# Causal branch of a two-layer backbone: norms one block ahead, turned keys' copies queued first, backward loads a block ahead, an update copied by ScalarE

## The chip, the cores and the metric

One core of a Trainium2 chip runs the whole program. The metric is device time in microseconds (us) of one execution. A core has a matrix engine (TensorE, PE in the profile; PEld are its weight loads), VectorE (DVE), ScalarE (ACT), GpSimd (POOL) and SyncE (SP), which here issues all the DMAs. Each engine works through its own queue in order and waits at its head.

## The reference

Two layers run over 2048 latent and 256 context tokens of width 1024. A layer normalises its tokens, modulates them, projects them to 3584 columns, runs four branches, and projects back with a gated residual. The branch that the change touches is a recurrence with 4 heads of 64 keys and 64 values, run once forward and once backward over the tokens, context first:

```
def step(state, inp):                       # one chunk of 64 positions
    a = jnp.cumsum(lf, axis=2)              # running log of the forget gate f
    s_new = exp(a_last) * state + einsum("bhsk,bhsv->bhkv", kc * exp(a_last - a), vc)
    inter = einsum("bhtk,bhkv->bhtv", qc * exp(a), state)
    dec = exp(where(causal, diff, -inf))    # diff = a at t minus a at s, causal: s <= t
    scores = einsum("bhtk,bhsk,bhtsk->bhts", qc, kc, dec)
    return s_new, inter + einsum("bhts,bhsv->bhtv", scores, vc)
```

The sum of both directions goes through an RMS norm per head. Inputs, weights and output are float32.

## The kernel before

Tokens are handled in 18 tiles of 128 rows, two to a block, so in 9 blocks; block 0 is the context. The kernel is written with a scheduling layer: the program is traced in an order, and a compile-time scheduler then sorts the instructions of every engine's queue by that order and by its own estimate of when each is ready. What is traced earlier has priority. Waits between engines are semaphores that the layer adds; two engines never use one PSUM bank at the same time. The traced order comes from `weave` (L41): each stream is a generator with a count of units and a span, and the stream whose next unit has the lowest relative place goes next. `after(i)` (L94) puts what is traced inside it behind instruction `i` on `i`'s own engine.

The stages of a layer that matter here:

1. **The forward stage** (L1427 to L1464; in layer 0 about 75 to 375 us of the trace, in layer 1 about 1434 to 1748 us). For each block `sb`, three streams are woven: `hg_proj(sb)` projects the block's queries, two directions' forget gates and values (L441 to L443 and L455 to L457, three fp16 products for one float32 product); `hg_levels(sb-1)` works on the block before; and `norms(sb)` normalises the two tiles of the block two ahead, in the span 0.3 to 1.0. Two blocks' tiles, 2 to 5, are normalised ahead of the loop (L1450 and `run(norms(0))`). A norm of one tile is `norm_front` (load L329 into one of two buffers `nh`, square on ScalarE L332, scaling on VectorE L336) and `norm_turn` (two groups of four TensorE transposes L353, each followed by four ScalarE modulations L360, then a cast L364 and a difference L365 on VectorE).
2. **Within `hg_levels`** keys K and queries Q are multiplied by products of forget gates over spans of 1, 2, 4, ..., 64 positions (levels `B`). At each level VectorE multiplies one half of the columns (L600, L603) and ScalarE copies the other half (L606, L607, "level copies", four for keys and queries together). TensorE forms scores from pairs of levels (`hg_scores`, L716), which are evacuated into Sd and Sx (L559 to L564). Then, for each of the block's two 128-row chunks `ch`: four TensorE transposes of the keys (L649), a ScalarE copy of them to SBUF (`kut`, L651, "key copy", one buffer), the products keys times values of both directions (L664) and the outputs (L673) into two PSUM banks `po` of the tag `sc`, which has two in all. The banks are then emptied: ScalarE copies outputs (L689), VectorE updates the forward state (`hg_state`, L475, two instructions), copies the backward direction's update to `dsb` (L692) and the gate product (L693), and adds the second bank (L695). Outputs and backward queries are stored to DRAM (L696, L697). The products L664 of the second chunk need the second key copy and both banks free.
3. **The last block** of the forward stage is woven with two blocks of `gate_block` for weight column 13 (48 products each, L455 to L457).
4. **The backward stage** (`hg_reverse`, about 375 to 470 us and 1745 to 1835 us): for each block, in the order 0, 8, 7, ..., 1, it loads stored queries (L739) and outputs (L740), multiplies the queries by the state (L750), updates the state (L475), adds, normalises and stores (L771). It is woven with the other gate blocks, Fourier blocks, weight preparation and, in layer 0, with modulation columns of 1 MB weight loads.

Of the kernel before, what the change touches and what calls it, by code (L numbers as in the profile page):

```python
# [12 lines left out]
F32 = mybir.dt.float32  # L13
# [13 lines left out]
NTT = NT // 128  # L27
KC = D // 128
DEPTH = 2
# [11 lines left out]
def weave(*streams):  # L41

    live = []
    for n, gen, *span in streams:
        a, b = span or (0.0, 1.0)
        live.append([0, n, gen, a, b - a])
    while live:
        e = min(live, key=lambda x: x[3] + x[4] * (x[0] + 0.5) / x[1])
        try:
            next(e[2])  # L50
            e[0] += 1
        except StopIteration:
            live.remove(e)
# [6 lines left out]
def run(gen, n=None):  # L60

    for i, _ in enumerate(gen):
        if i + 1 == n:
            break
# [8 lines left out]
class Net:  # L73
# [388 lines left out]
    def hg_open(self, l, keep):  # L462
        nc = self.nc

        self.hst = [self.t(keep, [128, 2, 64], F32, f"hst{i}", 1) for i in range(3)]
        for s in self.hst:
            nc.gpsimd.memset(s, 0.0)
        self.hcur = 0
        self.dsb = self.t(keep, [128, NTT, 2, 64], F32, "dsb", 1)
        self.fbc = self.t(keep, [128, NTT, 2], F32, "fbc", 1)  # L470

# [58 lines left out]
    def hg_levels(self, l, sb, hp):  # L530

        nc = self.nc
# [36 lines left out]
        while B <= 64:  # L569
            D_ = N // B  # L570

            F2 = self.t(hp, [128, 3 * (D_ // 2) + 8], F32, f"hF{2 * B}", 1)
            nc.vector.tensor_mul(
                out=F2[:, : 3 * D_ // 2], in0=F[:, 0 : 3 * D_ : 2], in1=F[:, 1 : 3 * D_ : 2]
            )
            if need and len(group) == 2:
                if pend:
                    keep()
                pend = self.hg_scores(group)
                group = []  # L580

            def fpair(base, step, n):

                v = F[:, base : base + 2 * step].rearrange("p (r q) -> p r q", r=2)
                return v[:, :, 0 : 4 * (n - 1) + 1 : 4].rearrange("p r n -> p n r")

            if B < 64:
                n4 = N // (4 * B)
                for X, Y, tag, (ob, os), (ib, is_) in (
                    (Kc, Ky, "hK", (1, D_ + 1), (D_, D_ + 3)),  # L590
                    (Qc, Qy, "hQ", (D_ + 1, D_ + 1), (0, D_ + 3)),
                ):
                    if X is None:
                        continue
                    Xn = self.t(hp, [128, N], F32, tag + "c", 3)
                    Yn = self.t(hp, [128, N], F32, tag + "y", 2)
                    v4 = lambda a: a.rearrange("p (n j b) -> p n j b", j=4, b=B)
                    x4, y4, xn, yn = v4(X), v4(Y), v4(Xn), v4(Yn)
                    sh = [128, n4, 2, B]
                    nc.vector.tensor_tensor(  # L600
                        out=xn[:, :, 0::3], in0=x4[:, :, 0::3], in1=fpair(ob, os, n4).unsqueeze(3).to_broadcast(sh), op=ALU.mult
                    )
                    nc.vector.tensor_tensor(  # L603
                        out=yn[:, :, 1:3], in0=x4[:, :, 1:3], in1=fpair(ib, is_, n4).unsqueeze(3).to_broadcast(sh), op=ALU.mult
                    )
                    nc.scalar.copy(out=xn[:, :, 1:3], in_=y4[:, :, 1:3])  # L606
                    nc.scalar.copy(out=yn[:, :, 0::3], in_=y4[:, :, 0::3])  # L607
                    if tag == "hK":
                        Kc, Ky = Xn, Yn
                    else:  # L610
                        Qc, Qy = Xn, Yn
                if need:
                    group.append((2 * B, Kc, Qc))
            else:
                res = []
                v2 = lambda a: a.rearrange("p (n j b) -> p n j b", j=2, b=64)
                fv = lambda d, e: F[:, d * D_ : d * D_ + D_].rearrange("p (n j) -> p n j", j=2)[:, :, e].unsqueeze(2).to_broadcast([128, 4, 64])
                for X, Y, tag, spec in (
                    (Kc, Ky, "hK", ((0, 0, 1), (1, 1, 0))),
                    (Qc, Qy, "hQ", ((1, 0, 0), (0, 1, 1))),  # L620
                ):
                    if X is None:
                        res += [None, None]
                        continue
                    for (half, d, e), tg in zip(spec, ("c", "y")):
                        Z = self.t(hp, [128, N], F32, tag + tg, 3 if tg == "c" else 2)
                        nc.vector.tensor_tensor(out=v2(Z)[:, :, half], in0=v2(X)[:, :, half], in1=fv(d, e), op=ALU.mult)
                        nc.scalar.copy(out=v2(Z)[:, :, 1 - half], in_=v2(Y)[:, :, 1 - half])
                        res.append(Z)
            F = F2  # L630
            B *= 2
            yield
            if B > 2:
                yield
# [7 lines left out]
        for ch in range(2):  # L642
# [5 lines left out]
                    x = (i * 2 + g) * 128  # L648
                    nc.tensor.transpose(pt[:, x : x + 128], c4(a, g), self.id32)  # L649
            kut = self.t(hp, [128, 512], F32, "hkut", 1)  # L650
            nc.scalar.copy(out=kut, in_=pt)  # L651
            yield
            yield

# [13 lines left out]
            if need:  # L668
# [19 lines left out]
                            mm(a, b, h, (Sd if a == b else Sx)[p, h % 2, ch * 2 + h // 2], it[p, ch, h * 64 : h * 64 + 64], h == 3)  # L688
                nc.scalar.copy(out=dv[:, ch], in_=po[0][:, 0:256])  # L689
            u = po[0][:, 256:512].rearrange("p (d g v) -> p d g v", d=2, g=2)  # L690
            self.hg_state(new, old, FC[:, 0, :, ch], u[:, 0])
            nc.vector.tensor_copy(out=self.dsb[:, tt], in_=u[:, 1])  # L692
            nc.vector.tensor_copy(out=self.fbc[:, tt], in_=FC[:, 1, :, ch])  # L693
            if need:
                nc.vector.tensor_add(out=dv[:, ch], in0=dv[:, ch], in1=po[1][:, 0:256])  # L695
# [27 lines left out]
    def hg_reverse(self, l, pool):  # L723
# [7 lines left out]
        for s in st:  # L731
            nc.gpsimd.memset(s, 0.0)
        cur = 0
        for sb in [0] + list(range(NTT // 2 - 1, 0, -1)):
            need = l < DEPTH - 1 or sb > 0
            if need:
                qb = self.t(pool, [128, 2, 256], F32, "hKc", 2)
                o = self.t(pool, [128, 2, 256], F32, "hQc", 2)
                nc.sync.dma_start(out=qb, in_=self.d_qb[sb * 2 : sb * 2 + 2].rearrange("c p x -> p c x"))  # L739
                nc.sync.dma_start(out=o, in_=self.d_op[sb * 256 : sb * 256 + 256].rearrange("(c p) x -> p c x", p=128))  # L740
                po = self.bank("pv", cols=1024)
            for ch in (1, 0):
                tt = sb * 2 + ch
# [647 lines left out]
    def layer(self, l, L, R, tail):  # L1391
# [35 lines left out]
        with ExitStack() as st:  # L1427
            hp = self.pool(st, "hg", "left")
            self.hin = {}
            block = self.hg_proj(l, 0, hp)  # L1430
            if l == 0:
                w = [self.wprep(l, b, quick=True) for b in (8, 9, 10)]
                with self.after(last):
                    run(w[0], 2)
                    run(w[1], 2)
                    run(w[2], 1)
                run(block, 8)
                for i in range(3):
                    run(w[i])
                    with self.after(*self.wlast):  # L1440
                        if i == 0:
                            run(w[2], 1)
                        run(block, 1 if i == 0 else 8)
                self.load_masks()
            else:
                self.wlast = ()
            self.hg_open(l, hgk)
            nc.gpsimd.memset(self.omx, 0.0)
            with self.after(*self.wlast):
                for tt in (2, 3):  # L1450
                    self.norm_tile(l, tt, nm)

            def norms(sb):
                for tt in (2 * sb + 4, 2 * sb + 5):
                    if tt < NTT:
                        h = self.norm_front(l, tt, nm)
                        yield
                        yield from self.norm_turn(l, tt, h, nm)

            run(block)  # L1460
            run(norms(0))
            for sb in range(1, NS):
                weave((33, self.hg_proj(l, sb, hp)), (22, self.hg_levels(l, sb - 1, hp)), (8, norms(sb), 0.3, 1.0), *([(7, self.wprep(l, 13), 0.4, 0.8)] if sb == NS - 1 else []))
            weave((22, self.hg_levels(l, NS - 1, hp)), chain(*gates(13, 512, some[:2])))  # L1464


        def late():
# [17 lines left out]
        with ExitStack() as st:  # L1485
            rp = self.pool(st, "rv", "left")
            streams = [
                (NS, self.hg_reverse(l, rp)),
                chain(*gates(13, 512, some[2:]), *[(9, self.fourier_block(sb, 12)) for sb in some]),
                (21, preps((12, 6, 4))[1], 0.1, 1.0),  # L1490
            ]
            if l == 0:
                streams.append((33, self.adaln_rest(self.pool(st, "ada", "left")), 0.1, 1.0))
            weave(*streams)
# [210 lines left out]
```

## Time and profile before

| | |
|---|---|
| median of 3 runs | 2701.15 us (2696.48 to 2701.3) |
| profiled execution, its own time | 2704.5 us |
| its span in the trace | 2701.9 us |
| PE busy | 2559.8 us, 95% of the span |
| PEld / DVE / ACT / POOL busy | 1914.5 / 2168.8 / 1476.1 / 106.1 us |
| mean granted TensorE clock | 0.982 |

The span is the time from the first to the last instruction of the program; the profiled execution's own time is 2.6 us longer. An engine's busy time is the union of its instructions, so TensorE is not idle for more than about 142 us in all.

### The profile page before, as it was taken

The numbers are of one execution on the slowest core, as the hardware profiler recorded it, in microseconds if no ns is written. First come the engines' busy times: TensorE is split into PE (matmuls) and PEld (weight loads), VectorE is DVE, ScalarE is ACT, GpSimd is POOL, SyncE is SP. The second block draws the span as 40 slices with busy tenths as digits, with TensorE's granted clock in tenths as the row PEclk, the third lists the DMA queues.
The fourth block names the chain that finished last, engine by engine and source line by source line (L and its number), as shares of the span: only waits on it lengthen the run. The fifth ranks groups of instructions, "written<-read, shape, count | busy, mean of one in ns | idle before, by whom it ended". The sixth has DMA issues, their size and how long they took to land. (4 is left out here: it accounts for less than half of the span.)

```text
span 2701.9 us, 67158 instructions
## 1 busy us (share of the span) xinstructions
PE 2559.8 (95%) x28046; PEld 1914.5 (71%) x28046; DVE 2168.8 (80%) x4771; ACT 1476.1 (55%) x2725; POOL 106.1 (4%) x108
## 2 busy tenths in 40 slices
PE   5899999999899999999999999999998999999998
PEld 3788877878777775555547788888886777555553
DVE  5888865677689889987878888778788988998875
ACT  2877642322225556788847666433221555798882
POOL 0000001001000000000000000010110000000000
PEclk7999999999999999999999999999999999999999
DMA  6111158353331005242372111243434100424325
GB/s 220 57 49 49 38 161 275 124 150 102 99 81 44 25 25 148 81 117 85 102 208 85 45 49 36 87 131 130 140 100 109 40 25 17 122 59 126 110 63 140
DMA packets 268679, 260.31 MB, mean 96 GB/s; under 512 B 95316, under 2 KB 237656, under 8 KB 268376
## 3 DMA queue, kind: packets, MB, share of 16 engines
q1 hardware_dynamic: 268376, 256.04, 31.8%
q8 instruction: 219, 3.59, 0.6%
q14 instruction: 84, 0.69, 0.1%
HBM read 168.59 MB, written 67.13 MB: 87 GB/s over the span
## 5 line engine op out<-in xcount | busy, mean ns | idle before, releaser
L441 PE MATMUL psmm<-xh,wh 128*128 128x256 f16 x2208 | 607.5, 275 | 10.3 <-DVE xh L364 6.1
L442 PE MATMUL psmm<-xl,wh 128*128 128x256 f16 x2208 | 606.2, 275 | 1.6 <-DVE xl L365 1.6
L443 PE MATMUL psmm<-xh,wl 128*128 128x256 f16 x2208 | 606.2, 275 | 0.9 <-DVE wl L417 0.9
L1034 ACT ACTIVATE aP<-pssc,pshift,ascale 128x512 f32<-128x512 f32 (+1 forms) x584 | 447.9, 773 | 242.8 <-PE pssc L1032 207.2
L455 PE MATMUL psmm<-wh,xh 128*128 128x256 f16 x1664 | 459.3, 276 | 10.3 <-ACT av L828 8.6
L457 PE MATMUL psmm<-wh,xl 128*128 128x256 f16 x1664 | 458.9, 276 | 0.0
L456 PE MATMUL psmm<-wl,xh 128*128 128x256 f16 x1664 | 458.7, 276 | 0.0
L1041 DVE TENSOR_TENSOR apl<-aP,aph 128x512 f16<-128x512 f32 (+1 forms) x584 | 394.0, 681 | 79.7 <-ACT aph L1040 74.4
L957 DVE TENSOR_REDUCE amx<-pstr 128x1 f32<-128x512 f32 (+1 forms) x648 | 390.1, 627 | 45.9 <-PE pstr L956 44.0
L998 PE MATMUL pspv<-V,aph 128*128 128x129 f16 x2320 | 289.6, 221 | 0.1
L999 PE MATMUL pspv<-V,apl 128*128 128x65 f16 x2320 | 267.5, 193 | 10.5 <-DVE apl L1041 9.8
L1040 ACT CAST aph<-aP 128x512 f16<-128x512 f32 (+1 forms) x444 | 269.3, 613 | 10.9
L999 PEld LDWEIGHTS <-apl 128*128 128x128 f16 x2320 | 207.5, 98 | 82.4 <-DVE apl L1041 27.8
L442 PEld LDWEIGHTS <-wh 128*128 128x128 f16 x2208 | 217.5, 99 | 66.3 <-issue 11.1
L441 PEld LDWEIGHTS <-wh 128*128 128x128 f16 x2208 | 217.7, 99 | 65.3 <-issue 12.4
L998 PEld LDWEIGHTS <-aph 128*128 128x128 f16 x2320 | 214.4, 97 | 57.9 <-ACT aph L1040 1.4
L956 PE MATMUL pstr<-K,Q 128*128 128x512 f16 (+1 forms) x648 | 228.4, 357 | 17.5 <-DVE amx L957 7.3
L443 PEld LDWEIGHTS <-wl 128*128 128x128 f16 x2208 | 217.3, 98 | 37.2 <-issue 2.6
L1031 PE MATMUL pssc<-Q,K 128*128 128x512 f16 (+1 forms) x584 | 220.4, 377 | 8.1 <-ACT aP L1034 6.6
L1032 PE MATMUL pssc<-Q,K 66*128 66x512 f16 (+1 forms) x584 | 221.0, 379 | 0.0
L1321 PE MATMUL psmm<-xh,oyh 128*128 128x512 f16 x544 | 207.9, 382 | 7.6 <-DMA oyh<-oa 5.6
L1321 PE MATMUL psmm<-xl,oyh 128*128 128x512 f16 x544 | 207.9, 382 | 0.0
(308 smaller groups left out, 4249.9 us busy)
## 6 DMA issues: line engine op xcount, KB each, us to landing
wst<-w_in SPq DMA_DIRECT2D x56, 512.0 KB
wmod<-w_mod SPq DMA_DIRECT2D x18, 1024.0 KB
d_G<-nh SPq DMA_DIRECT2D x51, 256.0 KB
oo<-d_O SPq DMA_DIRECT2D x34, 384.0 KB
og<-d_G SPq DMA_DIRECT2D x34, 384.0 KB
d_h<-oh SPq DMA_DIRECT2D x18, 512.0 KB
nh<-d_h SPq DMA_DIRECT2D x18, 512.0 KB
nh<-x SPq DMA_DIRECT2D x16, 512.0 KB
```

The lines of the kernel that those rows point to most:

```text
L441: nc.tensor.matmul(out, lhsT=wh[:, k, cs], rhs=a, start=(k == 0), stop=False)
L442: nc.tensor.matmul(out, lhsT=wh[:, k, cs], rhs=b, start=False, stop=False)
L443: nc.tensor.matmul(out, lhsT=wl[:, k, cs], rhs=a, start=False, stop=(k == KC - 1))
L455: nc.tensor.matmul(out, lhsT=a, rhs=wh[:, k, :], start=(k == 0), stop=False)
L456: nc.tensor.matmul(out, lhsT=a, rhs=wl[:, k, :], start=False, stop=False)
L457: nc.tensor.matmul(out, lhsT=b, rhs=wh[:, k, :], start=False, stop=(k == KC - 1))
L957: nc.vector.tensor_reduce(out=mx[:, h, j, i : i + 1], in_=ps[:, :w], axis=AX.X, op=ALU.max)
L998: nc.tensor.matmul(pv(j), lhsT=ph[:, t], rhs=self.V[:, s, kv, :], start=st, stop=False, skip_group_check=True)
L999: nc.tensor.matmul(pv(j)[:, 0:65], lhsT=pl[:, t], rhs=self.V[:, s, kv, 0:65], start=False, stop=sp and j % 2 == 1, skip_group_check=True)
L1034: nc.scalar.activation(out=P[:, :n], in_=ps[:, :n], func=AF.Exp, scale=self.ascale, bias=self.pshift)
L1041: nc.vector.tensor_sub(out=pl[:, :n], in0=P[:, :n], in1=ph[:, :n])
L1321: nc.tensor.matmul(ps, lhsT=y, rhs=w, start=(i == 0), stop=(i == len(mms) - 1))
```

## The change

Four things change. The norms of a block are traced one block ahead of their use instead of two, so that only tiles 2 and 3 are normalised ahead of the loop, and within a block they take the span 0.05 to 0.75 instead of 0.3 to 1.0. The level copies of the first two levels of a block are queued on ScalarE behind the last key copy of the block before. The copy of the backward update (`dsb`) goes from VectorE to ScalarE, ahead of the state update. In the backward stage the loads of a block are traced one block earlier, with a unit of their own ahead of the first block. A third gate block moves from the backward stage into the weave of the last forward block.

```
-        self.hcur = 0
+        self.hcur, self.kutlast = 0, []
...
-                    nc.scalar.copy(out=xn[:, :, 1:3], in_=y4[:, :, 1:3])
-                    nc.scalar.copy(out=yn[:, :, 0::3], in_=y4[:, :, 0::3])
+                    with self.after(*self.kutlast) if B < 4 else ExitStack():
+                        nc.scalar.copy(out=xn[:, :, 1:3], in_=y4[:, :, 1:3])
+                        nc.scalar.copy(out=yn[:, :, 0::3], in_=y4[:, :, 0::3])
...
-            nc.scalar.copy(out=kut, in_=pt)
+            self.kutlast = [nc.scalar.copy(out=kut, in_=pt)]
...
             u = po[0][:, 256:512].rearrange("p (d g v) -> p d g v", d=2, g=2)
+            nc.scalar.copy(out=self.dsb[:, tt], in_=u[:, 1])
             self.hg_state(new, old, FC[:, 0, :, ch], u[:, 0])
-            nc.vector.tensor_copy(out=self.dsb[:, tt], in_=u[:, 1])
...
-        for sb in [0] + list(range(NTT // 2 - 1, 0, -1)):
+        order = [0] + list(range(NTT // 2 - 1, 0, -1))
+
+        def load(sb):
+            if l == DEPTH - 1 and sb == 0:
+                return None
+            qb = self.t(pool, [128, 2, 256], F32, "hKc", 2)
+            o = self.t(pool, [128, 2, 256], F32, "hQc", 2)
+            nc.sync.dma_start(out=qb, in_=self.d_qb[sb * 2 : sb * 2 + 2].rearrange("c p x -> p c x"))
+            nc.sync.dma_start(out=o, in_=self.d_op[sb * 256 : sb * 256 + 256].rearrange("(c p) x -> p c x", p=128))
+            return qb, o
+
+        ahead = [load(order[0])]
+        yield
+        for i, sb in enumerate(order):
             need = l < DEPTH - 1 or sb > 0
+            if i + 1 < len(order):
+                ahead.append(load(order[i + 1]))
+            got = ahead.pop(0)
             if need:
-                qb = self.t(pool, [128, 2, 256], F32, "hKc", 2)
-                o = self.t(pool, [128, 2, 256], F32, "hQc", 2)
-                nc.sync.dma_start(out=qb, in_=self.d_qb[sb * 2 : sb * 2 + 2].rearrange("c p x -> p c x"))
-                nc.sync.dma_start(out=o, in_=self.d_op[sb * 256 : sb * 256 + 256].rearrange("(c p) x -> p c x", p=128))
+                qb, o = got
                 po = self.bank("pv", cols=1024)
...
             def norms(sb):
-                for tt in (2 * sb + 4, 2 * sb + 5):
+                for tt in (2 * sb + 2, 2 * sb + 3):
...
             run(block)
-            run(norms(0))
             for sb in range(1, NS):
-                weave((33, self.hg_proj(l, sb, hp)), (22, self.hg_levels(l, sb - 1, hp)), (8, norms(sb), 0.3, 1.0), *([(7, self.wprep(l, 13), 0.4, 0.8)] if sb == NS - 1 else []))
-            weave((22, self.hg_levels(l, NS - 1, hp)), chain(*gates(13, 512, some[:2])))
+                weave((33, self.hg_proj(l, sb, hp)), (22, self.hg_levels(l, sb - 1, hp)), (8, norms(sb), 0.05, 0.75), *([(7, self.wprep(l, 13), 0.4, 0.8)] if sb == NS - 1 else []))
+            weave((22, self.hg_levels(l, NS - 1, hp)), chain(*gates(13, 512, some[:3])))
...
-                (NS, self.hg_reverse(l, rp)),
-                chain(*gates(13, 512, some[2:]), *[(9, self.fourier_block(sb, 12)) for sb in some]),
+                (NTT // 2 + 1, self.hg_reverse(l, rp)),
+                chain(*gates(13, 512, some[3:]), *[(9, self.fourier_block(sb, 12)) for sb in some]),
```

## Rows read from the trace of the kernel before

**Rows 1.** Stretches: start:end, us, busy us of each engine (instructions), granted clock, DMA share, GB/s
```profile
80.00:375.00 295.00, 282.06 (x5348) 245.09 (x5347) 242.92 (x601) 205.41 (x532) 9.91 (x18) 0.99 0.17 54
375.00:470.00 95.00, 91.46 (x1048) 71.55 (x1046) 54.55 (x132) 25.97 (x46) 11.64 (x7) 0.96 0.86 277
...
1420.00:1745.00 325.00, 305.23 (x5177) 258.96 (x5175) 273.91 (x726) 208.47 (x512) 10.30 (x19) 0.98 0.17 54
1745.00:1835.00 90.00, 87.21 (x980) 76.32 (x978) 60.90 (x144) 27.30 (x48) 13.11 (x8) 0.98 0.46 144
```

**Rows 2.** Stretches of single blocks, layer 1: one with norms, one without
```profile
1519.70:1555.20 35.50, 33.28 (x587) 28.65 (x583) 29.73 (x79) 23.63 (x62) 1.10 (x2) 0.93 0.16 47
...
1656.60:1687.20 30.60, 30.47 (x591) 26.52 (x590) 25.24 (x71) 16.23 (x41) 0.00 (x0) 1.00 0.17 54
```

**Rows 3.** TensorE's waits, 75 to 375 us: who, for whom, total us, times, longest
```profile
PE pssc L664 <- DVE dsb L692: 4.4, 5, 1.4
PE pstr L353 <- DVE nh L336: 4.1, 3, 2.5
PE pspv L716 <- DVE hSd L564: 2.8, 3, 1.7
PE pssc L664 <- ACT hkut L651: 0.9, 1, 0.9
```

**Rows 4.** TensorE's waits, 1434 to 1748 us
```profile
PE pssc L664 <- ACT hkut L651: 9.7, 5, 2.2
PE pspv L716 <- DVE hSd L564: 6.6, 4, 3.3
PE pstr L353 <- ACT nt L360: 2.1, 1, 2.1
```

**Rows 5.** Timeline of TensorE at that block's end: start, us, line, what, times, idle before
```profile
1548.32 0.60 PE L353 MATMUL pstr<-id,nh 128*128 128x128 f32 x4
1548.75 0.38 PE L649 MATMUL pstr<-id,hKc 128*128 128x128 f32 x2
1548.97 0.38 PE L649 MATMUL pstr<-id,hKy 128*128 128x128 f32 x2
...
1553.54 1.12 PE L664 MATMUL pssc<-hi,hkut 128*64 128x64 f32 x16 [2.22 <-ACT hkut L651]
```

**Rows 6.** Timeline of ScalarE at the same place
```profile
1546.29 0.46 ACT L606 COPY hKc<-wst 128x256 f32<-128x256 f32 x1 [0.82 <-DVE wst L519]
...
1546.96 1.50 ACT L360 ACTIVATE nt<-pstr,modh,mods 128x128 f32<-128x128 f32 x4
...
1551.23 0.37 ACT L689 COPY wst<-pssc 128x256 f32<-128x256 f32 x1
1551.49 1.52 ACT L360 ACTIVATE nt<-pstr,modh,mods 128x128 f32<-128x128 f32 x4
1552.88 0.61 ACT L651 COPY hkut<-pstr 128x512 f32<-128x512 f32 x1
```

**Rows 7.** Timeline of VectorE at the same place
```profile
1551.85 0.48 DVE L475 SCALAR_TENSOR_TENSOR hst<-hst,hF,pssc 128x64 f32<-128x64 f32 x2
1552.24 0.30 DVE L692 COPY dsb<-pssc 128x128 f32<-128x128 f32 x1
```

**Rows 8.** Stretches at a low granted clock
```profile
379.10:386.00 6.90, 5.64 (x54) 4.26 (x55) 5.84 (x13) 0.63 (x1) 1.36 (x1) 0.51 1.08 365
...
1553.00:1560.00 7.00, 6.46 (x148) 5.62 (x152) 6.24 (x21) 4.35 (x12) 0.55 (x1) 0.76 0.06 21
```

**Rows 9.** VectorE's wait for a bank that ScalarE reads, 1434 to 1748 us
```profile
DVE hst L475 <- ACT wst L689: 3.2, 1, 3.2
```

**Rows 10.** TensorE's wait in layer 0's backward stage, 375 to 470 us
```profile
PE pspv L750 <- DMA hQc<-d_op: 3.5, 1, 3.5
```

**Rows 11.** Layer 0, queries of the second level and the scores that use them, timelines
```profile
226.36 0.42 DVE L600 TENSOR_TENSOR hQc<-hQc,hF 128x256 f32<-128x256 f32 x1
...
231.08 1.16 PE L716 MATMUL pspv<-hQc,hKc 64*64 64x64 f32 x64
```

## The prediction

> **What bounds the kernel now.** I read the page's table of busy times first, then the stretches of the stages that the diff touches, then TensorE's list of waits in each, and last the timelines of three engines around one such wait. The stretches say that TensorE is the bound in both forward stages and both backward stages: it is busy 282 of 295 us and 305 of 325 us forward, 91 of 95 and 87 of 90 us backward, and no other engine comes near [rows 1]. The edits take no TensorE work away, so the most they can win is TensorE's idle time in these stretches and what a fallen clock costs there.
>
> The lists of waits say where that idle time is. In layer 0 it is 4.4 + 0.9 us before L664, 4.1 us at the norm's transposes and 2.8 us at the scores [rows 3]; in layer 1 it is 9.7, 2.1 and 6.6 us for the same three [rows 4]. A block of layer 1 with norms takes 35.5 us, one without 30.6 [rows 2]. Eight transposes for each of two tiles are four groups of 0.60 us [rows 5], 2.4 us of that difference; the wait of 2.2 us at L664 is most of the rest.
>
> The timelines show how that wait comes about. The second chunk's key transposes end at 1549.35 and TensorE waits until 1553.54 with its next step, though it has filler for part of that [rows 5]. ScalarE meanwhile does a level copy of the next block (1546.29), four norm modulations (1546.96), the output copy of the first chunk (1551.23), four modulations more (1551.49) and only then the key copy (1552.88) [rows 6]. So the key copy comes 3.5 us after its data, and the first chunk's output copy, on which VectorE's emptying of the bank (1551.85) hangs [rows 7], is just as late.
>
> **Key copies and norms (term A).** Queueing the first two levels' copies behind the key copy takes them out of its way, and the new span (0.05 to 0.75) takes the norms of a block away from its end, where the key copies stand. With both gone, the copy can start at about 1549.4 and end 0.6 us later, before TensorE's filler is used up. I count the three L664 terms as gone: 4.4 + 0.9 + 9.7 = 15.0 us [rows 3, 4]. The clock is a second part: after the wait of rows 5 the granted clock is 0.76 over 7 us, so 3.4 us at 1.2 instead of 2.4 GHz, with TensorE busy, a loss of 1.7 us [rows 8]; layer 1 has one more such stretch behind such a wait, so 3.4 us. Term A is 18.4 us; it is nothing if the waits only change hands.
>
> **The copy of the update (term 0).** On VectorE it takes 0.30 us [rows 7]; on ScalarE it isn't in the trace. The nearest row is the output copy from the same bank with twice the columns, 0.37 us [rows 6]; the bounds are 0 and 0.37, and I take 0.37. Two per block are 0.7 us on an engine that is busy 23.6 of 35.5 us [rows 2], which hides it; where it does not, 36 of them are 13 us. VectorE loses 36 x 0.30 = 11 us of work, none of it on the bound by itself. What matters is the bank: VectorE's state update once waited 3.2 us for ScalarE's copy of the same bank [rows 9]. So the new copy stands ahead of the update, and the bank is free at about the old time: 0.37 for 0.30. The Trainium skill has this as a rule (PSUM — Partial Sum Buffer, section "PSUM bank collisions raise a hardware error"): reads of one bank by ScalarE and VectorE at the same time are an error, so they must be kept apart. If the two could run side by side, up to 18 second chunks x 0.30 = 5.4 us would be won; by the rule, with which the trace agrees, nothing.
>
> **Norms one block ahead (term D).** Two tiles fewer are ahead of the loop. TensorE's waits there, 4.1 and 2.1 us at L353, are for tiles 4 and 5 [rows 3, 4]; but in layer 0 the first projection of block 1 also waits for tile 3, so of the 4.1 us I count 1 as won, and of the 2.1 us 2. The other side: the pair's transposes do not vanish but come back in block 7, which had no norms. Four groups of 0.60 us per layer [rows 5] are added there; about half of them lay in waits ahead of the loop and cost nothing, so 2 x 1.2 = 2.4 us are lost. Net 0.6 us won; bounds 6.2 won to 4.8 lost. What is late next: the tiles must be ready when the next block's projection begins. In the old order the second tile's last modulations start at 1551.49 in a block that ends at 1555.2 [rows 2, 6]; a quarter of 35 us earlier leaves some 9 us for the rest of the norm, which is enough. A norm also issues its load, on SP, now ahead of the block before's stores, and its power on POOL, which is busy 10 of 295 us and has nothing else queued there; the load still needs the buffer of the tile two before, and with a DMA share of 0.17 in the stage it lands in time [rows 1].
>
> **Last forward block (term C).** TensorE waits 2.8 + 6.6 us for score evacuations [rows 3, 4], most of it in the last block, where there is no projection left to fill with. A third gate block is half as much filler again, taken from a stage that is bound by TensorE anyway, so the move itself costs nothing. I count half of 9.4 us, 4.7; bounds 0 and 9.4.
>
> **Backward loads (term B).** In layer 0 TensorE waits 3.5 us for the first block's outputs [rows 10], and behind that wait runs 6.9 us at clock 0.51, 5.64 of them busy [rows 8], a loss of 2.8. With a unit of their own ahead of the first product, and gate work in between, both go: 6.3 us. For later blocks I count nothing, since no wait of L750 for a load stands in the lists: those loads are hidden already. SP's stores and the 1 MB weight loads stand in the same queue; a load that waits for a buffer would hold them, but the buffer it needs is the one of two blocks before. Bounds 0 and 6.3.
>
> **New waits (term E).** What leaves the end of a block goes to other places in it: four groups of modulations of 1.5 us [rows 6] now stand beside score copies. If in every fourth block one of them is in the way, that is 14 / 4 x 1.5 = 5.3 us lost (14 blocks with norms). Bounds 0 and 21, one group in every block.
>
> **Sum.** 18.4 + 0.6 + 4.7 + 6.3 - 5.3 = 24.7 us. The profiled execution took 2704.5 us, so 2679.8 us, **2680**. That execution stands 3.3 us above the median of the three runs, within their spread of 4.8; against the median the forecast is 21 us less.
>
> **Rivals.**
>
> *R1, the wait changes hands.* L664 also needs the bank, and VectorE empties it at 1551.85 to 1552.3 [rows 7], only 1.2 us before TensorE started. In layer 0 it is VectorE, not the key copy, that is named for 4.4 of 5.3 us [rows 3]. If VectorE goes on doing the next block's levels first, A wins only 0.9 + 9.7 / 2 = 5.8 us and no clock, and if the filler does not help either, C is nothing: 5.8 + 0.6 + 6.3 - 5.3 = 7.4 won, 2697 us. For it: those names. Against it: the next block's second level needs copies that are now later, so VectorE has less to do first.
>
> *R2, slower: the level copies come too late for the scores.* They now wait for the second key copy, which waits for TensorE's transposes; behind it on ScalarE stand eight level copies, the value copy (L526), the next norm's square and then the score copies, and the next scores and VectorE's products of the third level wait for those. The first moves from 1546.29 to about 1550.0, 3.7 us. In layer 0 the second level's queries end at 226.78 and their scores start at 231.08, 4.3 us of slack [rows 11]. Below that delay the cost is nothing; if the chain loses more, for instance because the key transposes themselves come later, TensorE waits at L716 in every block. Price: half of the 4.3 us, 2.1 us, x 16 blocks (those followed by another) = 34 us, and it replaces E: 2704.5 - 30.0 + 34 = 2709; with the whole 4.3 us, 2743. I take 2715, nearer to the lower. For it: a slack so near to the delay. Against it: the compile-time order knows of the edge and can put projection work ahead of the scores, and VectorE, not the copies, paces the levels there.
>
> *R3, the loads ahead do nothing.* The order of the queues already put them early; then the first load still starts when the stage starts and B is nothing: 2686 us. For it: no later block waits for a load.
>
> *R4, all of it goes.* No new waits, and C whole: 24.7 + 5.3 + 4.7 = 34.7 won, 2670 us.
>
> **Chances.** Forecast 0.40, R1 0.24, R2 0.18, R3 0.09, R4 0.09. A measurement of this kernel can tell about 0.2%, 5.4 us, from no change. The forecast, R3 and R4 are all faster (0.57 of their 0.58, the rest the same), of R1 0.10 are faster and 0.13 the same, of R2 0.02 the same and 0.16 slower; with 0.01 of R1 slower that is 0.67, 0.16 and 0.17. The range for 8 in 10 reaches below R4 to 2663, and over R1 and the lower half of R2 to 2711. The forecast's own range is 2670 to 2692.
>
> **What would show it.** A: the list of waits for L664 shrinks from 15 us to under 4, the key copy starts within 1 us of its transposes, and layer 1's blocks with norms take 32 to 33 us. D: block 7 is about 2 us longer, block 1 shorter. C: waits at L716 in the last blocks fall under 5 us. B: no wait of L750 for a DMA in layer 0, and no low clock at its start. Update copy: ScalarE rows of 0.3 us and VectorE's state update right behind them. The prediction is wrong if L664 names VectorE with 8 us or more (R1), or if L716 waits in the middle blocks (R2), or if a wait of the projection for a tile's norm appears at the start of blocks.

## The result, and the profile after

The changed kernel takes 2679.18 us (median of 4 runs, 2677.28 to 2681.4), the kernel before 2699.69 us in the same session (4 runs): a ratio of 0.9926, 95% interval 0.9909 to 0.9943. The profiled execution took 2680.5 us, its span is 2678.2 us, 23.7 less than before. The medians are 20.5 us apart: the profiled execution of the kernel before stands 4.8 us above this median, that of the changed kernel 1.3, so some 3 of the 23.7 us belong to the two executions and not to the change. The forecast was 2680.

The page of the changed kernel, its busy times (share of the span, instructions):

```profile
PE 2562.4 (96%) x28046; PEld 1914.6 (71%) x28046; DVE 2161.5 (81%) x4735; ACT 1482.9 (55%) x2761; POOL 111.5 (4%) x108
```

TensorE's work is the same; VectorE has 36 instructions less, ScalarE 36 more. So the time can only have come from idle time and clock. Its stages, in the columns of [rows 1]; each window begins and ends at the same TensorE instruction, by count, as the window of before:

```profile
78.50:370.10 291.60, 284.66 (x5350) 246.98 (x5352) 237.81 (x576) 209.18 (x550) 12.66 (x16) 0.98 0.17 52
370.10:461.00 90.90, 87.91 (x1058) 68.73 (x1051) 51.64 (x131) 25.15 (x47) 11.18 (x9) 1.00 0.90 293
461.00:491.00 30.00, 28.10 (x294) 19.14 (x292) 15.45 (x46) 7.25 (x14) 3.78 (x3) 0.94 0.44 140
1413.90:1718.70 304.80, 302.06 (x5175) 258.05 (x5177) 268.35 (x702) 211.58 (x530) 11.97 (x17) 1.00 0.18 55
1718.70:1808.50 89.80, 84.74 (x994) 73.44 (x987) 61.88 (x148) 27.36 (x48) 13.85 (x10) 0.99 0.47 153
```

The third window is new. Before, the same stretch was:

```profile
470.00:496.40 26.40, 26.31 (x294) 18.56 (x293) 12.50 (x40) 7.35 (x14) 3.27 (x2) 1.00 0.43 136
```

Layer 1's forward stage gives 20.2 us (325.0 to 304.8): TensorE's idle time in it falls from 19.8 to 2.7, and its clock rises from 0.98 to 1.00. Layer 0's gives 3.4: 6.0 us of idle time go, but TensorE is busy 2.6 us longer, as its clock falls from 0.99 to 0.98. Layer 0's backward stage gives 4.1 and the 30 us behind it take 3.6 back; layer 1's gives 0.2. So nearly all of the gain is in the forward stages, and five sixths of it in one.

TensorE's waits in the changed kernel, layer 0 forward (75 to 368 us), answering to [rows 3]:

```profile
PE pstr L353 <- DVE nh L336: 4.1, 3, 2.5
PE pssc L665 <- DVE wst L696: 1.7, 6, 0.3
...
PE pspv L717 <- DVE hSd L564: 0.5, 1, 0.5
```

and layer 1 forward (1430 to 1735 us), the whole list, answering to [rows 4]:

```profile
PE pspv L717 <- DVE hSd L564: 1.6, 2, 1.0
PE pstr L353 <- DVE nrv L176: 0.8, 1, 0.8
```

The products of keys and values (L665, before L664) waited 15.0 us and now wait 1.7; the scores (L717, before L716) 9.4 and now 2.1. The blocks of [rows 2], with norms, and the one that had none:

```profile
1504.20:1535.80 31.60, 31.60 (x615) 27.75 (x608) 29.11 (x76) 23.86 (x64) 2.15 (x2) 1.00 0.16 52
1630.60:1662.20 31.60, 31.60 (x616) 27.74 (x609) 28.81 (x75) 21.86 (x60) 0.00 (x0) 1.00 0.12 36
```

TensorE works all of the 31.6 us at full clock. The end of the first of these blocks, where [rows 5 to 7] are of before: TensorE, ScalarE, VectorE.

```profile
1532.21 0.38 PE L650 MATMUL pstr<-id,hKy 128*128 128x128 f32 x2
...
1534.50 0.69 PE L665 MATMUL pssc<-hi,hkut 128*64 128x64 f32 x16
```
```profile
1531.69 0.27 ACT L692 COPY dsb<-pssc 128x128 f32<-128x128 f32 x1
1532.68 0.59 ACT L652 COPY hkut<-pstr 128x512 f32<-128x512 f32 x1 [0.72 <-PE pstr L650]
1533.16 0.44 ACT L607 COPY hKc<-wst 128x256 f32<-128x256 f32 x1
```
```profile
1533.47 0.55 DVE L573 TENSOR_TENSOR hF<-hF 128x384 f32<-128x384 f32 x1
1533.94 0.41 DVE L696 TENSOR_TENSOR wst<-wst,pssc 128x256 f32<-128x256 f32 x1
1534.28 0.46 DVE L475 SCALAR_TENSOR_TENSOR hst<-hst,hF,pssc 128x64 f32<-128x64 f32 x2
```

The key copy starts as the transposes end, not 3.5 us later. ScalarE itself waits 0.72 us for them, and no modulation stands near. The level copies (L607) follow it. VectorE has done the first level and starts to empty the bank at 1533.94. TensorE's own work between 1532.6 and 1534.50 is the next projection: the filler lasts.

### The profile page after: what moved, and what is told of

The parts are those of the page before. It is cut to its first block, busy times and chain, and to the rows that moved or that the text cites. A ratio compares the mean times of both kernels' runs of the same rounds, so it can differ in the third digit from the quotient of the medians.

```text
span 2678.2 us, 67249 instructions
## 1 busy us (share of the span) xinstructions
PE 2562.4 (96%) x28046; PEld 1914.6 (71%) x28046; DVE 2161.5 (81%) x4735; ACT 1482.9 (55%) x2761; POOL 111.5 (4%) x108
## 5 line engine op out<-in xcount | busy, mean ns | idle before, releaser
L441 PE MATMUL psmm<-xh,wh 128*128 128x256 f16 x2208 | 609.6, 276 | 10.2 <-DVE xh L364 6.1
L443 PE MATMUL psmm<-xh,wl 128*128 128x256 f16 x2208 | 608.7, 276 | 1.4 <-DVE wl L417 1.4
L441 PEld LDWEIGHTS <-wh 128*128 128x128 f16 x2208 | 218.7, 99 | 65.2 <-issue 12.6
L443 PEld LDWEIGHTS <-wl 128*128 128x128 f16 x2208 | 218.0, 99 | 39.1 <-issue 2.7
```

Of the source, the lines that this page charges most:

```text
L441: nc.tensor.matmul(out, lhsT=wh[:, k, cs], rhs=a, start=(k == 0), stop=False)
L443: nc.tensor.matmul(out, lhsT=wl[:, k, cs], rhs=a, start=False, stop=(k == KC - 1))
```

## The experiments

Each stands beside runs of the kernel before (0.2% is 5.4 us); "changed" is the changed kernel. The change is five edits, not four: the norms (distance and span), the queue order of the level copies, the copy of the update, the early loads, and the third gate block.

| kernel | median, us | ratio to before, interval |
|---|---|---|
| before + norms edit (order and span) | 2692.73 | 0.9963 [0.9951, 0.9975] |
| before + span alone | 2692.89 | 0.9960 [0.9946, 0.9974] |
| before + queue edit | 2696.84 | 0.9984 [0.9975, 0.9992] |
| before + norms + queue | 2682.51 | 0.9926 [0.9913, 0.9939] |
| changed, norms as before | 2690.37 | 0.9961 [0.9946, 0.9976] |
| changed, no queue edit | 2687.38 | 0.9942 [0.9930, 0.9955] |
| changed, old span only | 2694.26 | 0.9975 [0.9962, 0.9987] |
| changed, two blocks ahead only | 2682.81 | 0.9927 [0.9914, 0.9939] |
| changed, update copy on VectorE | 2678.28 | 0.9918 [0.9899, 0.9938] |
| changed, loads as before | 2681.43 | 0.9925 [0.9906, 0.9945] |
| changed, two gate blocks | 2680.92 | 0.9922 [0.9904, 0.9939] |
| changed + two repairs | 2684.72 | 0.9932 [0.9918, 0.9945] |

**Which of the two edits of the forward stage?** The norms edit taken out of the changed kernel, and put alone into the kernel before:

```
-                for tt in (2 * sb + 2, 2 * sb + 3):
+                for tt in (2 * sb + 4, 2 * sb + 5):
...
+            run(norms(0))
...  (8, norms(sb), 0.05, 0.75)  ->  (8, norms(sb), 0.3, 1.0)
```

> The changed kernel with the norms put back: two blocks ahead of use, span 0.3 to 1.0, tiles 4 and 5 ahead of the loop. Theory P (as predicted: the key copies are late because of both the level copies and the norm's modulations in front of them on ScalarE): with the modulations back at the block's end, waits at the key-value products (L664 before) come back to 5 to 10 us of the 15.0 in the kernel before, and of the 21 us won 7 to 12 are given back, about 2690 us. Rival N (the move of the norms does nearly everything, the queueing nothing): the waits come back to 13 us or more and 17 us or more are given back, 2697 us or more. Rival Q (the queueing does it all): under 3 us are given back, 2682 us or less.

> The kernel before with the norms alone changed (one block ahead, span 0.05 to 0.75). Theory P: the two parts add up, 7 to 12 us are won of 21, about 2690 us, and layer 1's waits at the key-value products fall from 9.7 us to 3 to 6. Rival N: 15 us or more are won, 2685 us or less, and these waits are gone. Rival Q: under 3 us are won.

And the queue edit, out and alone:

```
-                    with self.after(*self.kutlast) if B < 4 else ExitStack():
-                        nc.scalar.copy(...)
+                    nc.scalar.copy(...)
```

> The changed kernel without the order of the level copies behind the key copies. Theory P: the level copies come in front of the key copy again; waits at the key-value products of 3 to 8 us, and 4 to 9 us are given back, about 2686 us. Rival N: nothing changes, 2677 to 2682 us, waits at these products under 3 us as in the changed kernel. Rival Q: the old waits return, 15 us and more given back.

> The kernel before with the order of the level copies behind the key copies alone. Theory P: 4 to 9 us are won of 21, about 2693 us, with waits at the key-value products of 6 to 11 us. Rival N: under 2 us are won, or some are lost, since the norm's modulations still stand in front of the key copies. Rival Q: 15 us or more are won. Rival S (the slower one of the prediction): the scores (L716) wait in the middle blocks, more than the 9.4 us of the kernel before in all, and the kernel is no faster.

Alone, the norms edit wins 0.37% and the queue edit 0.16%; without one or the other, the changed kernel keeps 0.39% and 0.58%. Together (the row "before + norms + queue") they win 0.74%, more than the two alone add up to (0.53%), and that interval stands clear of the one of the norms alone; so both are needed. Taken out of the changed kernel, the norms edit costs clearly; the interval without the queue edit (0.9942) overlaps with that of the changed kernel. The traces show why. With the queue edit and late norms, TensorE's waits in layer 1's forward stage (1420 to 1735 us; the three largest) are mostly for scores:

```profile
PE pspv L717 <- DVE hSd L564: 8.3, 7, 2.9
PE pssc L665 <- DVE wst L696: 2.4, 4, 1.0
PE pstr L353 <- ACT nt L360: 2.1, 1, 2.1
```

Around the longest of them, that kernel's TensorE, VectorE and ScalarE:

```profile
1486.84 1.99 PE L717 MATMUL pspv<-hQc,hKc 64*64 64x64 f32 x64 [2.85 <-DVE hSd L564]
```
```profile
1485.06 0.75 DVE L336 TENSOR_SCALAR nh<-nh,nrr 128x1024 f32<-128x1024 f32 x1 [0.73 <-POOL nrr L178]
1485.73 0.42 DVE L600 TENSOR_TENSOR hQc<-hQc,hF 128x256 f32<-128x256 f32 x1
1486.07 0.72 DVE L564 COPY_PREDICATED hSd<-masks,pspv 128x512 f32<-128x512 uint16 x1
```
```profile
1483.00 1.05 ACT L332 ACTIVATE xl<-nh 128x1024 f16<-128x1024 f32 x1
1483.96 0.19 ACT L332 ACTIVATION_READ_ACCUMULATOR xl<-nh 128x1 f32 x1
1484.05 0.56 ACT L559 COPY hSd<-pspv 128x512 f32<-128x512 f32 x1
```

The norm's square (L332) stands ahead of the first copy of the scores (L559), and on VectorE the norm's scaling (L336) ahead of the masked one (L564); VectorE stands 0.73 us for GpSimd's power with the scores behind it. The Trainium skill (PSUM — Partial Sum Buffer, section "Engine vs sequencer instructions") calls these engines' queues strictly first in, first out; the trace agrees. With the queue edit alone it is the same: the scores' waits in layer 1 are 11.4 us against 6.6 [rows 4], those of the products 4.0 against 9.7. So the edit trades one wait for another while the norms stand late. That is rival R2's wait, at a price that the key copies' gain still covers.

With the early norms and no queue edit, layer 1 is cured too (2.0 us at the scores, 0.6 at the products), but layer 0 (75 to 370 us) keeps R1's wait:

```profile
PE pssc L664 <- DVE hst L475: 6.4, 6, 1.1
```

One of the six, on VectorE, then ScalarE:

```profile
153.57 0.55 DVE L573 TENSOR_TENSOR hF<-hF 128x384 f32<-128x384 f32 x1
154.04 0.42 DVE L600 TENSOR_TENSOR hKc<-hKc,hF 128x256 f32<-128x256 f32 x1
154.38 0.42 DVE L603 TENSOR_TENSOR hQy<-hQc,hF 128x256 f32<-128x256 f32 x1
...
155.86 0.75 DVE L336 TENSOR_SCALAR nh<-nh,nrr 128x1024 f32<-128x1024 f32 x1 [0.50 <-POOL nrr L178]
156.53 0.47 DVE L475 SCALAR_TENSOR_TENSOR hst<-hst,hF,pssc 128x64 f32<-128x64 f32 x2
```
```profile
154.50 0.60 ACT L651 COPY hkut<-pstr 128x512 f32<-128x512 f32 x1
```

The key copy is done at 155.10, but VectorE, whose level copies came early, does the next block's second level (154.04, 154.38) and a norm's scaling first, and empties the bank at 156.53; TensorE starts at 157.14. In the changed kernel the copies that the second level needs stand behind the key copy (151.86 in the same block), and VectorE empties the bank before that level:

```profile
153.47 0.41 DVE L696 TENSOR_TENSOR wst<-wst,pssc 128x256 f32<-128x256 f32 x1
...
154.52 0.42 DVE L600 TENSOR_TENSOR hKc<-hKc,hF 128x256 f32<-128x256 f32 x1
```

TensorE waits 0.30 us for it there. The profiled execution without the queue edit took 2680.57 us, the fastest of six at a median of 2687.38, so it is read for which waits there are. The 4.7 us that its wait is longer than the 1.7 us of the changed kernel are close to what the ratios differ by (0.16%, 4.3 us).

**These two alone, and what of the norms edit counts.** The kernel before with both edits and none of the other three:

> The kernel before with the two edits norms (one ahead, share 0.05 to 0.75) and queue order of the level copies, without the copy to ScalarE, the third gate and the early loads. Theory A (these two are the whole change, and they need each other): 2677 to 2682, forward blocks of layer 1 at 31.6 us. Theory B (the parts add up: 10 us and 4 to 6 us of the 23 are theirs alone, the rest needs the other edits): 2684 to 2688.

0.9926: as far as these runs can tell, the two are the whole change. Then the span and the distance apart: the changed kernel with the old span (`0.3, 1.0`), the same with the old distance (tiles 2sb + 4 and + 5, `run(norms(0))`), and the kernel before with the new span only.

> The changed kernel with the norms still one block ahead, but spread over the share 0.3 to 1.0 of the block as before, not 0.05 to 0.75. Theory A (one block ahead only works if the norms end before the block does): the projection of each next block waits for VectorE's split of the last norm tile, 0.5 to 1 us in 13 blocks, 7 to 13 us slower, 2686 to 2692. Theory B (the projection's first products use other tiles long enough, or the next block begins with weight-side work): 2677 to 2682.

> The changed kernel with the norms two blocks ahead as before, but spread over the share 0.05 to 0.75 of the block. Theory A (what counts is where in the block the norms' ScalarE work stands, early, not for which block it is): like the changed kernel, 2677 to 2683, waits for the score tile in layer 1's forward stage at 2 us or less. Theory B (the distance counts: one block ahead takes the norms' work away from the last blocks' scores): like 'all but the norms', 2688 to 2692, with waits for the score tile of 8 us in layer 1.

> The kernel before with one thing changed: the norms, still two blocks ahead, are spread over the share 0.05 to 0.75 of the block instead of 0.3 to 1.0. Theory A (the place in the block is the whole of the norms edit): as 'the norms edit alone' on the kernel before, 2690 to 2695, its forward blocks of layer 1 at about 32 us instead of 33 to 35. Theory B (without the queue order of the level copies the distance counts after all): 2697 to 2703, blocks of layer 1 at 33 us or more.

The distance is worth nothing that these runs can tell (0.9927 against 0.9926), the span alone all that the norms edit wins alone (0.9960 against 0.9963). One block ahead with the late span is worse than the changed kernel by 0.49%, 13 us, for the next projection waits for the tiles (its two rows, layer 1, 1410 to 1735 us):

```profile
PE psmm L442 <- DVE xl L365: 7.7, 7, 2.0
PE psmm L441 <- DVE xh L364: 1.7, 1, 1.7
```

**The other three edits,** each taken back in the changed kernel. The update's copy:

```
-            nc.scalar.copy(out=self.dsb[:, tt], in_=u[:, 1])
             self.hg_state(new, old, FC[:, 0, :, ch], u[:, 0])
+            nc.vector.tensor_copy(out=self.dsb[:, tt], in_=u[:, 1])
```

> The changed kernel with the copy of the backward update put back on VectorE, after the state update. Theory A (the forecast's term 0: the copy's engine is worth nothing): within 3 us of the changed kernel's 2679, the waits of the products for VectorE at the block's last scores unchanged (1.7 us in layer 0, 0 in layer 1). Theory B (the copy stands in VectorE's queue ahead of what the next products wait for, so with the key copies early it has become the last wait): these waits grow by 2 to 4 us over the two layers, as they are larger by 2.5 us in 'queueing alone' (VectorE copies, 4.9) than in 'all but the norms' (ScalarE copies, 2.4), time 2682 to 2685.

The backward loads (L742, L743 moved back into the block that uses them, `NS` units):

> The changed kernel with the backward branch's loads put back into the block that uses them. Theory A (forecast, term B): the 3.5 us wait of TensorE for the reloaded partial output comes back in layer 0, with a low-clock stretch behind it: 6.3 us slower, 2685 to 2686. Theory B (the stage is fed by DMA: what the earlier load won there is given back to a later load of a modulation weight, on which TensorE waits 2.5 us in the changed kernel): the old wait comes back, that of the modulation weight goes, 2677 to 2681.

The third gate block (`some[:3]`, `some[3:]` to `some[:2]`, `some[2:]`):

> The changed kernel with two gate blocks beside the last forward block instead of three. Theory A (forecast, term C): half of the waits for the score tile come back, 4.7 us slower, about 2684. Theory B (by the traces, in which 7.3 us of these waits and the low clock behind them went): 8 to 10 us slower, 2687 to 2689. Theory C (the waits went because the norms no longer stand in ScalarE's queue there, and the third gate only moves TensorE work out of the backward stage): 2677 to 2681, the waits for the score tile at 2 us or less in both layers.

None of the three makes a difference that these runs can tell. With VectorE's copy the waits at L665 do grow, from 1.7 to 4.3 us over both layers, but that does not reach the median. With the old loads the old wait comes back (370 to 480 us),

```profile
PE pspv L751 <- DMA hQc<-d_op: 4.1, 1, 4.1
```

where the changed kernel has these (370 to 500 us; a fourth, of 0.5 us, is left out), the first two of them new:

```profile
PE pssc L268 <- DMA wmod<-w_mod: 2.5, 1, 2.5
PE pstr L142 <- DVE amax L302: 1.9, 1, 1.9
PE pstr L1152 <- DVE modrow L280: 1.9, 1, 1.9
```

It is the same in all the traces: the eight kernels with the early loads wait 1.4 to 2.5 us at L268 near the stage's start and 1.7 to 1.9 us at L142 near its end; the six without wait 2.8 to 4.1 us for the reloaded outputs, and 0.4 us at most for the `amax` of L142.

With two gate blocks the scores of layer 1's forward stage wait again, at 1410 to 1735 us and mostly in the last block,

```profile
PE pspv L717 <- DVE hSd L564: 4.7, 4, 2.9
```

against 1.6 us. Ahead of the last block (TensorE instruction 18000) this kernel is 6.5 us behind the changed one, behind the backward stage (22000) 4.7: what the last block loses is given back. Of the 6.5 us, 4.4 arose between instructions 10000 and 18000, where the edit changes nothing, so two executions can differ by that much. The backward stage's waits at L1171, L1152 and L443 (1735 to 1830 us) are 2.3 us with the gate block in it, 5.0 without.

**Two repairs.** The changed kernel, in layer 0's first block with the norms at 0.3 to 0.9, against the 2.5 us wait of L353; and with a third buffer for the reloaded outputs (and one less for the squares), so that SyncE's queue needn't hold a load for a store:

```
+    (8, norms(sb), 0.05 if l or sb > 1 else 0.3, 0.75 if l or sb > 1 else 0.9)
...
-            o = self.t(pool, [128, 2, 256], F32, "hQc", 2)
+            o = self.t(pool, [128, 2, 256], F32, "hQc", 3)
```

> The changed kernel with two things more: in layer 0's first forward block the norms spread over 0.3 to 0.9 instead of 0.05 to 0.75, and in the backward stage three buffers for the reloaded partial outputs (one for the squares), so that SyncE doesn't hold a load until a store has landed. Theory A (the two remaining waits are on TensorE's path): TensorE's wait of 2.5 us for the third norm tile and the 2.5 us for the modulation weight go, with half a low-clock stretch (1.7), 2672 to 2676. Theory B (the stage start is held by the weights' preparation, the backward stage by DMA in total): the waits change hands, 2677 to 2682.

No gain: the waits change hands, as theory B said (60 to 370 us):

```profile
PE psmm L441 <- DVE xh L364: 4.4, 1, 4.4
PE pstr L353 <- ACT nt L360: 3.1, 1, 3.1
```

No kernel that was run is measurably faster than the changed one.

## Why the prediction was right, and where it was not

**Term A** was right in mechanism and close in size. Forecast 18.4 us; of the L664 waits 13.3 us went (3.6 in layer 0, 9.7 in layer 1), and of the low-clock stretches both that it counted (3.4 us): 16.7. Against that, layer 0's forward stage was busy 2.6 us longer at a lower clock, which no term had. The reason was two things in one, and the experiments part them: the span took the norms out of the way of key copies and scores, and the queue edit kept VectorE from running ahead of the bank. Neither gives the whole without the other.

**Term E** was wrong: 5.3 us of new waits were forecast, and a middle block of layer 1 has none (31.60 us busy of 31.60). What the norms stand beside now is not on TensorE's path.

**Term B** failed in the step "both go: 6.3 us". The wait for the first block's outputs went and the low clock at its start with it, but not because the load came earlier. Before, it was issued 0.3 us into the stage:

```profile
375.28 0.47 SPq L740 DMA_DIRECT2D hQc<-d_op  x1
```

In the changed kernel it still stands in SyncE's queue behind the forward stage's last stores, and is issued 5.4 us into the stage, which begins at 370.1. SyncE, then TensorE:

```profile
375.46 0.47 SPq L743 DMA_DIRECT2D hQc<-d_op  x1
375.97 1.09 SPq L258 DMA_DIRECT2D wmod<-w_mod  x2
```
```profile
384.16 1.10 PE L268 MATMUL pssc<-wmod,cact 128*32 128x256 f32 x16 [2.47 <-DMA wmod<-w_mod]
385.96 0.69 PE L764 MATMUL pspv<-hst,hKc 64*64 64x64 f32 x32
464.60 0.27 PE L142 MATMUL pstr<-id,amax 128*1 128x128 f32 x1 [1.90 <-DVE amax L302]
```

TensorE does gate products first, has none left at 381.69, and then waits 2.5 us for a modulation weight, whose load is the next one in that queue; the kernel before came to this weight only at 390.06. The products that read the reloaded queries (L764) come only at 385.96. At the stage's end TensorE waits once more, for VectorE's `amax`, with the clock at 0.75 over the 6.9 us from 465.5; of the 4.1 us that the stage won, the 30 us from 461 take 3.6 back. With the loads put back, the kernel is no slower that could be told. I had named the rest of SyncE's queue in one clause and then priced it at nothing. What sets the time of that first product stays open, SyncE's queue, the DMAs' total (share 0.90) or VectorE: TensorE's weight loads for it name VectorE's `wam` (2.7 us), and with the third buffer the products' own wait does (1.4 us), at no gain in time.

**Term C**: the waits at the scores fell by 7.3 us, not 4.7; taking the gate back returns 5.0 of them, near the forecast's half, but the time hardly moves. What failed is "the move itself costs nothing": the backward stage has waits of its own, less of them with the gate block there.

**Term D** was right in size: I forecast 0.6 us for the distance, with the span counted under A, and two blocks ahead is no slower that could be told. One block ahead moves time about: layer 1's first block, from its first product at L441 to the next block's, falls from 28.7 to 25.0 us, and the one without norms rises from 30.6 to 31.6 (2 us were forecast). Of its parts, layer 1's 2.1 us at L353 went, as forecast, but layer 0's 4.1 us stand unchanged, so they were not for the tiles that are no longer there.

**Term 0** was right at nothing. The copy takes 0.27 us, between the bounds. The Trainium skill (VectorE: DVE Perf Modes, section "The TRN2 errata — SBUF-src ops pay a fixed extra latency per instruction") has a formula for ScalarE copies from PSUM, 172 cycles plus one per column at 1.2 GHz; by it 0.25, 0.36 and 0.57 us for 128, 256 and 512 columns, as an estimate, and the rows above and those of [rows 6] show 0.27, 0.37 and 0.59.

So the sum, 24.7 us, came out within 1 us of the span's gain by luck. By the experiments the two edits of the forward stage (terms A, D and E, forecast at 13.7 us) give 20 us, and the other three (terms B, C and 0, forecast at 11.0) nothing that the runs can tell: the first group was too low mostly by E, the second too high, and the two cancelled. The start helped as well, for the 24.7 us were taken from an execution above the median, and the medians differ by 20.5. The total says less for the reasoning than term A does. R1 and R2 did not happen in the changed kernel, but each is what happens when one half of the change is left out, and their reasons ("VectorE has less to do first"; a slack near the delay) were the right ones. R3's price for B came true, and its reason in part: the load was issued no earlier.

## What to carry to other kernels

Where one engine's queue holds work of three streams, ask of each piece not which block it belongs to but where in the block it stands: moving the norms from the end of the block to its start was worth 0.4%, a block's distance nothing that could be told. An order edge on one engine also paces the engine that feeds on it, for better (VectorE empties the bank first) and for worse (scores come late), so its price depends on what else stands there. A filler or a load that is moved into one stage is taken from another; look at that one's waits before counting the gain. Tracing a load earlier was worth nothing here, for it was issued no earlier: it still stood behind the stage before in its queue.

## What the runs showed that was not expected

A short wait was enough to go with a lower clock: before, the granted clock was 0.76 over the 7 us behind a single wait of 2.2 us [rows 5, 8], and with that stage's waits gone it is 1.00 throughout. Not every such wait goes with one: with the norms edit alone TensorE waits 3.3 us for scores in layer 1's last block (until 1712.4 us), and the clock is 1.00 over the 17 us from 1705. One profiled execution can stand well away from its kernel's median: that of "norms + queue" took 2689.55 us at a median of 2682.51, that of the two repairs 2676.22 at 2684.72, so these traces were read for their waits and not for their length.
